# Prompt attention with probabilities split into two fp16 parts by VectorE instead of fp32 words split and rejoined around a DMA transpose

## The chip, the cores and the metric

The kernel runs on one core of a Trainium2 chip. The metric is the device time of one execution in microseconds (us). A lower time is better. The profile shows one execution, with the busy intervals of TensorE (PE; its weight loads are PEld), VectorE (DVE), ScalarE (ACT), GpSimd (POOL), and the DMA queue that SyncE issues (SP).

## What is computed

One layer of a hybrid trunk over two groups of requests with shared weights: a prompt of 1024 tokens and eight samples of 16 tokens. After a modulated RMS norm, one projection gives q, k, v, gates and the inputs of a state-space branch (SSD). The change touches the attention of the prompt alone:

```python
def attend(q, k, v, bias, mask):
    s = jnp.einsum('bqhd,bkhd->bhqk', q, k).astype(jnp.float32) * (ATT_HEAD_DIM ** -0.5) + bias[None].astype(jnp.float32)
    s = jnp.where(mask, s, -1e30)
    p = jax.nn.softmax(s, axis=-1).astype(v.dtype)
    return jnp.einsum('bhqk,bkhd->bqhd', p, v)
```

There are 16 heads of 64 columns. A chunk of 64 query tokens sees itself and the 8 chunks before it, so a block of 128 queries works with at most 5 blocks of 128 keys. The output of attention is gated and projected, the SSD branch runs on the same normed input, both are merged, projected and added to the input.

## The kernel before

All 1152 tokens (1024 of the prompt, 128 of the samples) are worked through together. Large products are made from fp16 parts: an fp32 operand becomes a high part `hi` and a rest `lo`, and three fp16 matmuls replace one in fp32 (hi x hi, hi x lo, lo x hi). `halves` makes the parts (ScalarE the high one, VectorE the rest), and `level` sums squares of an operand into a column of `sums`. At the end every column is compared with a range; if one is outside, a flag makes the program run a second, general kernel behind this one.

The program is emitted by one loop, `run`. Its main stream are dense projections, in matmuls that stream 384 columns (`dense`, lines 409 to 412, and `dense_tok`, lines 462 to 464). Between them it puts the steps of other generators when a planned clock (`clock[0]`) and credits let them go; `until(t)` and `pause(t)` hold a generator to a planned time, and `late(...)` keeps an instruction in program order. Instructions of one engine run in their order; the hardware waits on semaphores.

Attention has 8 units of two heads each (`attention(u)`). A unit projects q, k, v for all tokens (`dense_gen`, evicted by `ev`), normalises and transposes q and k (`prelude`), and then runs `prompt` and `sample`. `prompt` has eight query blocks `m` of 128 tokens with `n = min(m, 4) + 1` key blocks, in six rounds (`ROUNDS`). A round first multiplies finished probabilities with v (`weigh`, line 1057), and then makes scores (line 1101) for one to three query blocks into PSUM; the two-bank tile `s` exists once, the one-bank tiles `g` three times. VectorE evacuates the scores with the bias and a running minimum (`negated`, line 1007). ScalarE exponentiates and sums (`exps`, line 1001). VectorE makes the reciprocal (line 1002) and scales the probabilities in fp32 (line 1004).

The probabilities must be transposed, keys onto partitions. `turn(m)` does it with the DMA transpose, which moves 2-byte elements: ScalarE copies the fp32 words into two planes of 16-bit halves (line 1034), the DMA transposes both planes (line 1036), and VectorE joins them to fp32 words again (line 1041). `weigh` then runs one fp32 matmul for each key block and head, with 64 columns of `v` as weights; the two heads write the two halves of the PSUM partitions. VectorE multiplies the result into the gate (line 1107). The sample's probabilities go through the same three steps (lines 1174, 1175, 1177).

Buffers are slots of one SBUF arena, by layouts: `L_ATT` for attention (tag "S" holds 10 buffers of 640 columns for scores and what is transposed, tag "T" whole rows of v and gates), `L_SSD` and `L_HEAD` for the SSD stage, and `L_MORE`, six further row buffers from column `E0` on, which SSD stages take first. `walloc` and `wpair` hold a generator until a slot is free.

Of the kernel before, what the change touches and what calls it, by code (L numbers as in the profile page):

```python
# [9 lines left out]
F16 = mybir.dt.float16  # L10
# [6 lines left out]
P = 128  # L17
# [42 lines left out]
SW = 2.0 ** 8  # L60
SA = 4.0
SM = 1.0
W_MEAN = (4.0, 1024.0)
X_MEAN = (0.25, 2.0 ** 19)

# [73 lines left out]
def trunk_kernel(ctx: ExitStack, tc: tile.TileContext, h, again):  # L139
# [80 lines left out]
    L_START["ada"] = L_START["ada"] + arena.set_layout(E0, [("ada", 8, 1024)])["ada"]  # L220
    L_MORE = arena.set_layout(E0, [("T", 6, 1184), ("H", 1, 1024)])
    L_SSD["H"] = L_SSD["H"] + L_MORE["H"]
    L_ST = rarena.set_layout(0, [("b", 4, P), ("s", 2, P), ("x", 2, 2 * P)])

    def alloc(lay, tag, cols):
        if lay is L_H or lay is L_W or lay is L_W3 or lay is L_Q:
# [654 lines left out]
    def attention(u):  # L881
# [4 lines left out]
        def dense_gen():  # L886
            qk = yield from walloc(lay, "Q", 16 * P)
            v = yield from walloc(lay, big, NT)
            nb = yield from walloc(lay, "n", 84)
            st["qk"], st["v"], st["nb"] = qk, v, nb  # L890
            if u == NU - 1:
                dts["raw"] = yield from walloc(lay, "T", NT)

            def ev(t, ps):

                while t == 8 and "turned" not in st:
                    blocked[0] = "q and k of the first tokens"
                    yield None
                c = qk.ap[:, 2 * (t % 8) * P:2 * (t % 8 + 1) * P]
                nc.scalar.activation(c, ps[:, :2 * P], AF.Copy, scale=1.0 / SW)  # L900
# [88 lines left out]
        def done():  # L989
            st["left"] -= 1  # L990
            att_left[0] -= 1
            if st["left"] == 0:
                dma(att_d[u], st["z"].ap)
                for n in ("z", "v"):
                    st[n].free()

        def exps(ps, sm_):

            n = len(ps)
            for e, p in enumerate(ps):  # L1000
                nc.scalar.activation(p, p, AF.Exp, bias=sm_[:, 4 + e:5 + e], scale=-1.0, accum_out=sm_[:, 6 + e:7 + e])  # L1001
            nc.vector.reciprocal(sm_[:, 8:8 + n], sm_[:, 6:6 + n])
            for e, p in enumerate(ps):
                nc.vector.tensor_scalar(p, p, sm_[:, 8 + e:9 + e], None, ALU.mult)  # L1004

        def negated(p, least, ps, bap, most=3.0e38):
            late(nc.vector.tensor_tensor_reduce(p, ps, bap, -1.0, most, ALU.add, ALU.min, least))  # L1007
# [1 line left out]
        def prompt():  # L1009
# [2 lines left out]
            qh, ql, kh, kl = st["ops"]  # L1012
            v, z, bias = (st[n] for n in ("v", "z", "bias"))

            place, turned, probs, tpt, mins = {}, {}, {}, {}, {}
            claimed = set()
            pairs = {0: 3, 1: 2, 2: 1, 3: 0}

            def turn(m):

                n = min(m, 4) + 1
                if pairs.get(m) in claimed:
                    yield from ready(lambda: m in turned)
                else:
                    claimed.add(m)
                    t = yield from wpair(lay, "S", 640)
                    for q, at in ((m, place[m][0][1]), (pairs.get(m), {0: 4 * P, 2: 2 * P}.get(pairs.get(m), 0))):
                        if q is not None:
                            turned[q] = [(b, at) for b in t]
                turning[0] -= 1  # L1030
                for e in range(2):
                    yield from until(probs[m] + 1000 * e)
                    (x, at), (y, _) = place[m][e], turned[m][e]
                    nc.scalar.activation(planes(y, at, n), words(x, at, n), AF.Copy)  # L1034
                    yield from until(probs[m] + 1000 * e + 900)
                    dma(x.ap[:, at:at + n * P].bitcast(U16).rearrange("p (i k) -> p i k", k=P),
                        y.ap[:, at:at + n * P].bitcast(U16), transpose=True)
                for e in range(2):
                    yield from until(probs[m] + 1000 * e + TURN)
                    (x, at), (y, _) = place[m][e], turned[m][e]  # L1040
                    nc.vector.tensor_copy(words(y, at, n), planes(x, at, n))  # L1041
                xs = place.pop(m)
                if pairs.get(m) not in place:
                    for x, _ in xs:
                        x.free()
                tpt[m] = clock[0] + 3500

            def weigh(js, po):

                cost = 200  # L1050
                for a, j in enumerate(js):
                    n = min(j, 4) + 1
                    for i in range(n):
                        for e in range(2):
                            vc = (j + 1 - n + i) * P + e * HD
                            x, o = turned[j][e]
                            late(nc.tensor.matmul(po[e * HD:e * HD + HD, a * P:(a + 1) * P], v.ap[:, vc:vc + HD],  # L1057
                                                  x.ap[:, o + i * P:o + (i + 1) * P], start=i == 0, stop=i == n - 1))
                    cost += 2 * n * 103
                for j in js:  # L1060
                    for x, _ in turned.pop(j):
                        if pairs.get(j) not in turned:
                            x.free()
                return cost

# [10 lines left out]
            for pieces, js in ROUNDS:  # L1076
# [27 lines left out]
                yield cost  # L1104
                if js:
                    ms = slice(js[0] * P, (js[-1] + 1) * P)
                    nc.vector.scalar_tensor_tensor(z.ap[:, ms], po, 0.5 / SW, z.ap[:, ms], ALU.mult, ALU.mult)
                t = clock[0] + 1000
                for m, c, w, k, o in pieces:
                    n = min(m, 4) + 1  # L1110
# [7 lines left out]
                    t += 4.4 * w  # L1118
                    if c + w == n * P:
                        exps([x.ap[:, at:at + n * P] for x, at in place[m]], sm_)  # L1120
                        mins.pop(m).free()
# [10 lines left out]
        def sample():  # L1132
# [6 lines left out]
            for bg in range(2):  # L1139
# [20 lines left out]
                    x.free()  # L1160
                negated(p.ap, sm_.ap[:, 4:5], sv[:, :640], bs.ap)
                exps([p.ap], sm_.ap)
                sm_.free()
                bs.free()
                yield 1400
# [2477 lines left out]
```

## Time and profile before

| | us |
|---|---|
| median of 3 runs | 1877.16 (1872.84 to 1878.64) |
| the profiled execution | 1871.97 |
| its span, first to last instruction | 1870.2 |
| TensorE busy in the span | 1781.9 (95%) |
| VectorE busy | 1210.7 (65%) |
| ScalarE busy | 1049.5 (56%) |

The mean granted TensorE clock was 0.991 of full speed. Matmuls are pipelined, so the busy time of a group of matmuls is the union of their intervals, and the duration of one contains its way through the array; the rate is seen from one start to the next. Idle time of an engine is put down to what released it last. A group's row gives line, engine, operation, tiles, shape and count, then busy us and mean ns of one, then the idle time before it.

### The profile page before, as it was taken

The page shows a single profiled execution, that of the slowest core. Times are in us where ns is not written, and L with a number is a line of the kernel's source. Part 1 is how long each engine was busy: PE and PEld are TensorE (multiplying, and loading weights), DVE is VectorE, ACT ScalarE, POOL GpSimd, SP SyncE. Part 2 cuts the span into 40 slices and gives each one's busy share as a digit, 9 for nine tenths or more (in the row PEclk, how much of TensorE's full clock was granted, in tenths as well). Part 3 has the DMA queues.
Part 4 walks back from the last instruction along what each step waited for, and adds up shares of the span by engine and source line. Part 5 has one row for each costly group of instructions (what it writes and reads, how often), then busy time and mean ns, then how long its engine had stood idle before and what let it go on. Part 6 is the DMA issues. An engine that isn't in the chain of part 4 may idle for free. (4 is left out here: it accounts for less than half of the span.)

```text
span 1870.2 us, 34169 instructions
## 1 busy us (share of the span) xinstructions
PE 1781.9 (95%) x13341; PEld 1114.3 (60%) x13341; DVE 1210.7 (65%) x2247; ACT 1049.5 (56%) x1999; POOL 350.0 (19%) x624
## 2 busy tenths in 40 slices
PE   7998998988989999999999999999999999999997
PEld 3655555554555555666666666566666656666664
DVE  7446657565675676776777787677664634888732
ACT  8866765666667667555655565465554623334520
POOL 0222313232232210121132213212212110000000
PEclk9999999999999999999999999999999999999999
DMA  9257767675676768453444435444456863331331
GB/s 382 92 125 191 157 178 171 173 178 149 166 194 176 168 150 181 128 168 104 120 152 140 134 116 159 127 127 122 136 168 207 325 205 97 109 97 46 98 123 53
DMA packets 266564, 284.84 MB, mean 152 GB/s; under 512 B 199628, under 2 KB 200664, under 8 KB 266392
## 3 DMA queue, kind: packets, MB, share of 16 engines
q1 hardware_dynamic: 257432, 253.90, 48.9%
q0 software_dynamic: 8960, 28.65, 4.0%
q8 instruction: 107, 1.75, 0.4%
q14 instruction: 65, 0.53, 0.1%
HBM read 192.70 MB, written 43.66 MB: 126 GB/s over the span
## 5 line engine op out<-in xcount | busy, mean ns | idle before, releaser
L409 PE MATMUL d<-arena 128*128 128x384 f16 x2172 | 711.4, 328 | 1.5 <-DVE arena L1408 1.3
L410 PE MATMUL d<-arena 128*128 128x384 f16 x2172 | 711.2, 327 | 0.0
L412 PE MATMUL d<-arena 128*128 128x384 f16 x2172 | 711.0, 327 | 0.0
L412 PEld LDWEIGHTS <-arena 128*128 128x128 f16 x2280 | 224.0, 98 | 148.2 <-issue 4.4
L409 PEld LDWEIGHTS <-arena 128*128 128x128 f16 x2280 | 223.9, 98 | 147.9 <-issue 10.5
L410 PEld LDWEIGHTS <-arena 128*128 128x128 f16 x2280 | 223.9, 98 | 142.7 <-issue 6.6
L319 ACT ACTIVATE arena<-arena 128x1024 bf16<-128x1024 f32 (+2 forms) x161 | 173.4, 1077 | 132.9 <-DMA arena<-in_wall_dram 109.9
L327 ACT ACTIVATE arena<-arena 128x1024 f16<-128x1024 f32 (+1 forms) x117 | 121.2, 1043 | 172.1 <-PE d L410 147.4
L1041 DVE COPY arena<-arena 128x1280 uint16<-128x1280 uint16 (+4 forms) x128 | 101.2, 791 | 140.6 <-DMA arena<-arena 125.6
L462 PE MATMUL d<-arena 128*128 128x384 f16 (+1 forms) x568 | 186.4, 329 | 1.9 <-ACT arena L665 1.6
L463 PE MATMUL d<-arena 128*128 128x384 f16 (+1 forms) x568 | 186.7, 329 | 0.0
L464 PE MATMUL d<-arena 128*128 128x384 f16 (+1 forms) x568 | 186.5, 329 | 0.0
L328 DVE SCALAR_TENSOR_TENSOR arena<-arena 128x1024 f16<-128x1024 f32 (+1 forms) x117 | 144.3, 1234 | 25.5 <-ACT arena L327 25.4
L1001 ACT ACTIVATE arena<-arena 128x640 f32<-128x640 f32 (+2 forms) x144 | 100.9, 703 | 102.8 <-DVE arena L1007 102.6
L1034 ACT ACTIVATE arena<-arena 128x1280 uint16<-128x1280 uint16 (+4 forms) x128 | 122.4, 995 | 46.2 <-DVE arena L1004 32.5
L1437 ACT ACTIVATE arena<-arena 128x128 f32<-128x128 f32 x288 | 88.3, 388 | 49.5 <-DMA arena<-acs_d 49.5
L1249 DVE SCALAR_TENSOR_TENSOR arena<-arena 128x1176 f32<-128x1176 f32 x72 | 104.6, 1453 | 5.6 <-ACT arena L1246 5.0
L928 POOL TENSOR_SCALAR arena<-arena 128x16 f32<-128x16 f32 (+1 forms) x24 | 8.5, 354 | 463.8 <-DVE arena L906 463.7
L1057 PE MATMUL g<-arena 128*64 128x128 f32 x960 | 67.9, 283 | 16.4 <-DVE arena L1041 7.6
L462 PEld LDWEIGHTS <-arena 128*128 128x128 f16 x576 | 56.7, 98 | 44.7 <-issue 9.8
L463 PEld LDWEIGHTS <-arena 128*128 128x128 f16 x576 | 56.4, 98 | 39.6 <-issue 5.2
L464 PEld LDWEIGHTS <-arena 128*128 128x128 f16 x576 | 56.5, 98 | 38.6 <-issue 2.5
(238 smaller groups left out, 2637.0 us busy)
## 6 DMA issues: line engine op xcount, KB each, us to landing
arena<-in_wall_dram SPq DMA_DIRECT2D x85, 512.0 KB
arena<-acs_d SPq DMA_DIRECT2D x32, 576.0 KB
arena<-in_kc_dram SPq DMA_DIRECT2D x64, 256.0 KB
arena<-in_vc_dram SPq DMA_DIRECT2D x64, 256.0 KB
arena<-in_wada_dram SPq DMA_DIRECT2D x24, 512.0 KB
arena<-in_xT_dram SPq DMA_DIRECT2D x16, 576.0 KB
gate_d<-arena POOLq DMA_DIRECT2D x48, 192.0 KB, 3.3
arena<-eacs_d SPq DMA_DIRECT2D x32, 288.0 KB
```

The source lines that it names most:

```text
L319: keep(nc.scalar.activation(junk[:, :n], x, AF.Square, scale=scale * n ** -0.5, accum_out=sums[:, c:c + 1]))
L327: keep(nc.scalar.activation(hi, x, AF.Copy, scale=scale))
L328: keep(nc.vector.scalar_tensor_tensor(lo, x, scale, hi, ALU.mult, ALU.subtract))
L409: nc.tensor.matmul(ps, hi.r[:, wc], kh.r[:, tok], start=k == 0, stop=False)
L410: nc.tensor.matmul(ps, hi.r[:, wc], kl.r[:, tok], start=False, stop=False)
L412: nc.tensor.matmul(ps, lo.r[:, wc], kh.r[:, tok], start=False, stop=k == nk - 1)
L462: nc.tensor.matmul(ps, kh.r[:, tok], wh, start=k == 0, stop=False)
L463: nc.tensor.matmul(ps, kh.r[:, tok], wl, start=False, stop=False)
L464: nc.tensor.matmul(ps, kl.r[:, tok], wh, start=False, stop=k == KT - 1)
L1034: nc.scalar.activation(planes(y, at, n), words(x, at, n), AF.Copy)
L1041: nc.vector.tensor_copy(words(y, at, n), planes(x, at, n))
L1249: nc.vector.scalar_tensor_tensor(yc, r.ap[:, j:j + n], w4[:, i, j:j + 1], yc, ALU.mult, ALU.add)
```

## The change

The scaling of the prompt's probabilities moves out of `exps` and into `turn`. There VectorE writes, for each head, the scaled probability times 2^12 as fp16 and the rest, computed in fp32 and rounded to fp16, behind it, into a second buffer; this buffer is transposed by DMA back into the one that held the fp32 scores. ScalarE's splitting copy and VectorE's joining copy are gone for the prompt; the sample keeps them. `weigh` runs three fp16 matmuls for each key block and head: high part of v with the high and the low part of the probabilities, low part of v with the high part. The fp16 parts of v are made in `ev` (by `halves`, in two pieces of 512 columns) and checked by `level`, which gives the range check eight more entries. They lie in a new layout `L_V`, 4 slots of 512 columns from `E0` on; four more buffers of tag "S" lie behind them, both over slots of `L_MORE`. The planned times in `turn` and the planned cost in `weigh` change with it.

```diff
-    NPART, NOPER = 121, 40
+    NPART, NOPER = 121, 48
...
+    L_V = arena.set_layout(E0, [("v", 4, NP // 2)])
+    L_ATT["S"] = L_ATT["S"] + arena.set_layout(E0 + 4 * NP // 2, [("S", 4, 640)])["S"]
...
+                if t in (4, 8):
+                    o = slice((t - 4) * P, t * P)
+                    halves(vh.r[:, o], vl.r[:, o], v.ap[:, o], 1.0)
+                    if t == 8:
+                        level(vh.r, 1.0, kind="x")
...
         def exps(ps, sm_):
-            n = len(ps)
             for e, p in enumerate(ps):
                 nc.scalar.activation(p, p, AF.Exp, bias=sm_[:, 4 + e:5 + e], scale=-1.0, accum_out=sm_[:, 6 + e:7 + e])
-            nc.vector.reciprocal(sm_[:, 8:8 + n], sm_[:, 6:6 + n])
-            for e, p in enumerate(ps):
-                nc.vector.tensor_scalar(p, p, sm_[:, 8 + e:9 + e], None, ALU.mult)
...
             def turn(m):
...
+                sm_ = mins.pop(m)
+                r = sm_.ap[:, 8:10]
+                yield from until(probs[m] - 1000)
+                nc.vector.reciprocal(r, sm_.ap[:, 6:8])
+                nc.vector.tensor_scalar(r, r, SP, None, ALU.mult)
+                ys = []
                 for e in range(2):
-                    yield from until(probs[m] + 1000 * e)
-                    (x, at), (y, _) = place[m][e], turned[m][e]
-                    nc.scalar.activation(planes(y, at, n), words(x, at, n), AF.Copy)
-                    yield from until(probs[m] + 1000 * e + 900)
-                    dma(x.ap[:, at:at + n * P].bitcast(U16).rearrange("p (i k) -> p i k", k=P),
-                        y.ap[:, at:at + n * P].bitcast(U16), transpose=True)
+                    x, at = place[m][e]
+                    p = x.ap[:, at:at + n * P]
+                    y = temp[m][e].ap[:, at:at + n * P].bitcast(F16)
+                    nc.vector.tensor_scalar(y[:, :n * P], p, r[:, e:e + 1], None, ALU.mult)
+                    nc.vector.scalar_tensor_tensor(y[:, n * P:], p, r[:, e:e + 1], y[:, :n * P], ALU.mult, ALU.subtract)
+                    ys.append(y)
+                sm_.free()
                 for e in range(2):
-                    yield from until(probs[m] + 1000 * e + TURN)
-                    (x, at), (y, _) = place[m][e], turned[m][e]
-                    nc.vector.tensor_copy(words(y, at, n), planes(x, at, n))
...
-                tpt[m] = clock[0] + 3500
+                    yield from until(probs[m] + 1000 + 1400 * e)
+                    x, at = place[m][e]
+                    dma(x.ap[:, at:at + n * P].bitcast(U16).rearrange("p (i k) -> p i k", k=P), ys[e].bitcast(U16), transpose=True)
+                yield from until(probs[m] + 2400 + TURN)
...
+                tpt[m] = clock[0]
...
             def weigh(js, po):
...
                     for i in range(n):
-                        for e in range(2):
-                            vc = (j + 1 - n + i) * P + e * HD
-                            x, o = turned[j][e]
-                            late(nc.tensor.matmul(po[e * HD:e * HD + HD, a * P:(a + 1) * P], v.ap[:, vc:vc + HD],
-                                                  x.ap[:, o + i * P:o + (i + 1) * P], start=i == 0, stop=i == n - 1))
-                    cost += 2 * n * 103
+                        o = slice((j + 1 - n + i) * P, (j + 2 - n + i) * P)
+                        for w, (v_, b) in enumerate(((vh, i), (vh, n + i), (vl, i))):
+                            for e in range(2):
+                                late(nc.tensor.matmul(po[e * HD:e * HD + HD, a * P:(a + 1) * P], v_.r[:, o.start + e * HD:o.start + e * HD + HD],
+                                                      xs[e][:, b * P:(b + 1) * P], start=i == 0 and w == 0, stop=i == n - 1 and w == 2))
+                    cost += n * 165
...
-                    nc.vector.scalar_tensor_tensor(z.ap[:, ms], po, 0.5 / SW, z.ap[:, ms], ALU.mult, ALU.mult)
+                    nc.vector.scalar_tensor_tensor(z.ap[:, ms], po, 0.5 / (SW * SP), z.ap[:, ms], ALU.mult, ALU.mult)
```

`SP` is 2^12. The sample's code scales its probabilities itself now, with the two instructions that stood in `exps`.

More of the change, by code (lines that the diff above doesn't have):

```diff
@@ L62 @@
 SM = 1.0
+SP = 2.0 ** 12
 W_MEAN = (4.0, 1024.0)
@@ L889, in dense_gen @@
             nb = yield from walloc(lay, "n", 84)
-            st["qk"], st["v"], st["nb"] = qk, v, nb
+            vh = yield from walloc(L_V, "v", NP)
+            vl = yield from walloc(L_V, "v", NP)
+            st["qk"], st["v"], st["nb"], st["v16"] = qk, v, nb, (vh, vl)
             if u == NU - 1:
@@ L1013, in prompt @@
             v, z, bias = (st[n] for n in ("v", "z", "bias"))
-            place, turned, probs, tpt, mins = {}, {}, {}, {}, {}
-            claimed = set()
+            vh, vl = st["v16"]
+            place, temp, probs, tpt, mins = {}, {}, {}, {}, {}
+            claimed, turned = set(), set()
             pairs = {0: 3, 1: 2, 2: 1, 3: 0}
@@ L1021, in turn @@
                 n = min(m, 4) + 1
[L1022 to L1025, printed above, removed]
+                if m not in claimed:
                     t = yield from wpair(lay, "S", 640)
-                    for q, at in ((m, place[m][0][1]), (pairs.get(m), {0: 4 * P, 2: 2 * P}.get(pairs.get(m), 0))):
-                        if q is not None:
-                            turned[q] = [(b, at) for b in t]
+                    for q in {m, pairs.get(m, m)}:
+                        claimed.add(q)
+                        temp[q] = t
@@ L1162, in sample @@
                 exps([p.ap], sm_.ap)
+                nc.vector.reciprocal(sm_.ap[:, 8:9], sm_.ap[:, 6:7])
+                nc.vector.tensor_scalar(p.ap, p.ap, sm_.ap[:, 8:9], None, ALU.mult)
                 sm_.free()
```

19 lines of the change are left out of this document (10 added, 9 removed).

## The prediction

> **What bounds the kernel now.** I read the page's head first, then the busy time by windows, split about where the attention ends. The columns are the stretch, its length, busy time of TensorE, weight loads, VectorE, ScalarE and GpSimd with instruction counts, granted clock, DMA share, GB/s.
>
> ```profile
> span 1870.2 us, 34169 instructions
> ...
> PE 1781.9 (95%) x13341; PEld 1114.3 (60%) x13341; DVE 1210.7 (65%) x2247; ACT 1049.5 (56%) x1999; POOL 350.0 (19%) x624
> ```
> ```profile
> 100.00:745.00 645.00, 588.81 (x4984) 350.73 (x4983) 409.89 (x1033) 426.92 (x889) 157.92 (x283) 0.98 0.69 168
> 745.00:1870.20 1125.20, 1106.13 (x7774) 713.00 (x7772) 744.89 (x1132) 542.90 (x963) 173.95 (x302) 1.00 0.44 136
> ```
> ```profile
> 466.00:473.50 7.50, 6.24 (x40) 3.86 (x40) 6.40 (x14) 5.27 (x7) 6.93 (x8) 0.54 0.82 180
> 673.00:745.00 72.00, 66.20 (x567) 41.11 (x566) 50.40 (x104) 52.44 (x88) 7.72 (x15) 1.00 0.67 156
> ```
>
> TensorE is the bound throughout, so whatever is taken from its work or its idle time moves the end. After 745 us it idles 19 us in 1125; during attention 645 - 588.8 = 56.2 us, and there the clock is 0.98 of full, worth 0.02 x 645 = 13 us. The loss comes in short pieces: from 466 to 473.5 us the clock was 0.54, right behind a wait. The waits show what TensorE waited for (total, times, longest):
>
> ```profile
> PE s L1101 <- DVE arena L1007: 18.0, 8, 3.2
> PE g L1186 <- ACT arena L900: 7.7, 4, 2.8
> PE g L1057 <- DVE arena L1041: 7.6, 6, 2.6
> ```
>
> The first is a score matmul that finds its PSUM bank not yet emptied by VectorE. The timeline shows one, and that it runs slowly afterwards: the same six score matmuls start 0.75 us before the next six here, 0.42 us in an undisturbed round.
>
> ```profile
> 306.58 0.33 PE L412 MATMUL d<-arena 128*128 128x384 f16 x1
> 306.75 0.33 PE L409 MATMUL d<-arena 128*128 128x384 f16 x1
> 309.55 0.98 PE L1101 MATMUL s<-arena 64*128 64x320 f16 x6 [2.48 <-DVE arena L1007]
> 310.30 1.04 PE L1101 MATMUL g<-arena 64*128 64x320 f16 x6
> ...
> 397.14 0.58 PE L1101 MATMUL s<-arena 64*128 64x320 f16 x6
> 397.56 0.57 PE L1101 MATMUL g<-arena 64*128 64x320 f16 x6
> ```
>
> **The products on TensorE.** Per pair of heads there are 1+2+3+4+4x5 = 30 blocks of 128 keys, 240 in all. Before, a block is one fp32 matmul for each head, in two halves of the array's columns at once, four records a block. The groups by form:
>
> ```profile
> L1057 PE MATMUL g<-arena 128*64 128x128 f32 x960 | 67.9, 283 | 16.4 <-DVE arena L1041 7.6 <-issue 4.1 <-DVE arena L1007 2.3
> ...
> L1545 PE MATMUL g<-arena 128*64 128x16 f32 x512 | 17.8, 207 | 0.0
> ```
> ```profile
> 366.98 0.75 PE L1101 MATMUL s<-arena 64*128 64x128 f16 x12
> 367.57 0.57 PE L1101 MATMUL g<-arena 64*128 64x320 f16 x6
> ```
>
> 67.9 us / 240 = 0.283 us a block, with the ends of the runs. After, a block is six fp16 matmuls, three pairs. No fp16 matmul with 64 weight columns is in the trace, so I bound a pair. From below: in the last fence twelve matmuls, six of 128 columns and six of 320, take 367.57 - 366.98 = 0.59 us; six of 320 take 0.42 (above), so three pairs of 128 columns take 0.17, 0.057 a pair. From above: L1545 has the weight shape of the change (128x64, two column halves) and next to nothing to stream; 17.8 us / 256 pairs = 0.070, which is what two such weight loads cost by themselves. I take 0.065, as the load is the nearer row: 0.195 a block, 0.22 with the ends of runs, 53 us in all, **15 us less**. Bounds 0.19 and 0.24: 22 and 10 less.
>
> The Trainium skill speaks against this: "TensorE: Matmul & The Clock Gate", section "Back-to-back issue gap", gives about 81 ns for each matmul of 128 columns in a stream of weight loads and matmuls. By it a block would be 6 x 0.081 = 0.49 us and the products an estimated 49 us longer. The pairs of 0.057 us above do not agree with it as long as two halves of the array overlap.
>
> **Work moved between VectorE and ScalarE.** Rows of the page and of the groups by form:
>
> ```profile
> L1041 DVE COPY arena<-arena 128x1280 uint16<-128x1280 uint16 (+4 forms) x128 | 101.2, 791 | 140.6 <-DMA arena<-arena 125.6
> ...
> L1034 ACT ACTIVATE arena<-arena 128x1280 uint16<-128x1280 uint16 (+4 forms) x128 | 122.4, 995 | 46.2 <-DVE arena L1004 32.5
> ```
> ```profile
> L328 DVE SCALAR_TENSOR_TENSOR arena<-arena 128x1024 f16<-128x1024 f32 x113 | 138.5, 1227 | 24.9 <-ACT arena L327 24.8
> L319 ACT ACTIVATE arena<-arena 128x1024 bf16<-128x1024 f32 x117 | 123.3, 1054 | 132.2 <-DMA arena<-in_wall_dram 109.9 <-DMA arena<-in_wssd_dram 10.7 <-DMA arena<-in_watt_dram 7.1
> L1001 ACT ACTIVATE arena<-arena 128x640 f32<-128x640 f32 x80 | 65.6, 820 | 85.6 <-DVE arena L1007 85.5
> L1631 DVE SCALAR_TENSOR_TENSOR arena<-arena 128x1152 f16<-128x1152 f32 x32 | 43.3, 1365 | 4.2 <-ACT arena L1629 4.2
> L1004 DVE TENSOR_SCALAR arena<-arena 128x640 f32<-128x640 f32 x80 | 41.4, 551 | 1.5
> L1007 DVE CUSTOM_DVE_ANT_0 arena<-g,arena 128x320 f32<-128x320 f32 x48 | 24.5, 544 | 0.0
> L1007 DVE CUSTOM_DVE_ANT_0 arena<-s,arena 128x320 f32<-128x320 f32 x48 | 21.4, 484 | 0.1
> L1002 DVE RECIPROCAL arena<-arena 128x2 f32<-128x2 f32 x64 | 10.2, 159 | 39.9 <-ACT arena L1001 39.9
> L1564 DVE TENSOR_TENSOR arena<-arena 128x512 f32<-128x512 f32 x16 | 11.0, 689 | 0.3
> ```
>
> ScalarE loses L1034, 122 us. It gains 16 fp16 copies of v of 512 columns (at most the 1.05 us of L319, 17 us) and 8 squares of 1024 (8.4 us): some 97 us less over the stage's 427. VectorE loses the copies behind the transpose, 101 us. It keeps the scaling (L1004, now writing fp16) and gains 128 subtractions. L328 and L1631 give (1365 - 1227)/128 = 1.08 ns an element, so 0.81 us at 640 columns and 0.26 to 0.68 at 128 to 512: 64 x 0.81 + 16 x 1.87 = 82 us. With 64 more tiny operations (0.16 each, 10 us) and 16 subtractions for v (0.69, 11 us) VectorE comes out 2 us up: no gain, no loss. The DMA transposes stay, as many and as large; their source is now written by VectorE, and TensorE waits for their landing itself.
>
> **Idle time.** In the built order of TensorE's instructions I count the 384-column dense matmuls (306.58 and 306.75 above are two in a row; the kernel plans 0.1625 us for one) between two uses of the score bank. Before, prompt scores follow sample scores by 44 and 22 of them; the 22 (3.6 us) is where 309.55 waits. After, it is 38 and 87. The tightest new distance is 18, from the scores of query block 7 to the next sample scores. So of the 18 us I let 15 go. L1057's wait for the copies goes, as the copy does; except in the last pair of heads the products come 81 or more dense matmuls (13 us) behind the scores that they need, more than the chain of 10.2 us worked out below: 6.5 of 7.6. The wait for L900 shrinks with ScalarE's load: 5 of 7.7. Together **26 us**, between 0 and 33. What is late next is VectorE's queue, where the scaling and subtraction of one block, 2 x (0.55 + 0.81) = 2.7 us, now stand between evacuations. With half of the longest waits gone, I let half of the clock loss go: **7 us** (0 to 13).
>
> **What the change costs: the last pair of heads.** The fp16 parts of v and four more score buffers lie where the first SSD tiles go. In the built order the dense matmuls run out there: after the scores of block 5 only 41 dense matmuls precede its products, and none stands between the scores of block 7 and the products of blocks 6 and 7 (before: 85 and 57). The chain then lies open. Its DMA part:
>
> ```profile
> 288.46 2.63 SPq L1036 DMA_TRANSPOSE arena<-arena  x2
> ...
> 291.78 0.75 DVE L1041 COPY arena<-arena 128x1024 uint16<-128x1024 uint16 x1 [1.20 <-DMA arena<-arena]
> 292.98 2.47 DVE L1041 COPY arena<-arena 128x1024 uint16<-128x1024 uint16 x1 [0.46 <-DMA arena<-arena]
> ```
>
> Two issues take 2.63 us and the second lands 292.98 - 291.09 = 1.9 us later. For block 7: evacuation 2 x 0.48 + 2 x 0.54 = 2.1; exponentials to 1.4 us later (the first of two of 0.82 overlaps the evacuation); reciprocal and scaling factor 0.3; scaling and first subtraction 2 x 0.55 + 0.81 = 1.9; issues 2.6 and landing 1.9: 10.2 us idle. Block 5 has 41 x 0.1625 = 6.7 us of dense matmuls and about 3 of others as cover: some 2 us idle. A wait three times the 3.2 us ahead of the window at 466 us costs at least its loss, 0.46 x 7.5 = 3.4 us; I take 3. In all **15 us more** (10 to 20); the 5.8 us that TensorE idles from 673 to 745 us today (72 - 66.2) are left as they are.
>
> **Sum.** -15 - 26 - 7 + 15 = -33 us. The profiled execution took 1872.0 us (span 1870.2 and 1.8 around it), so 1839 by its own time; the median of the runs shown is 1877.2, so **1844 us** there. Favourable ends: -22 - 33 - 13 + 10 = -58, 1819. Unfavourable: -10 - 0 - 0 + 20 = +10, 1887. A measurement of this kernel cannot tell less than about 0.3%, 5.6 us, from no change.
>
> **Rivals.** *The idle time does not fall.* VectorE stays first in, first out and 410 us busy of 645; the new reciprocals still wait for exponentials (39.9 us in L1002's row), and new waits replace the old ones. Then -15 + 15 = 0: 1877, give or take 10. For it: VectorE's load is unchanged. Against: 125.6 us of its waiting for transposes (L1041's row) go.
>
> *Slower: the halves of the array do not overlap in fp16.* Each of the six matmuls of a block then takes a pair's time, 6 x 0.065 = 0.39 us, 94 us for 240, 26 more instead of 15 less: -33 + 41 = +8, 1885, and with the upper bound of 0.07, 1892. The point from which it decides: the products alone lose above 0.283/3 = 0.094 us a pair, the whole change above (67.9 + 18)/240/3 = 0.119. Against it: in L1057 and L1545 the halves overlap in fp32.
>
> The Trainium skill, "TensorEngine Tiling", section "Restrictions and Gotchas", says that column tiling excludes fast weight load, which is one way to this rival. No run here shows fp16 weights in column halves.
>
> *The change does not do what it says.* Its range check gets eight more entries, one for each v; if one failed, the second kernel in the program would run as well, which at least doubles the time.
>
> **Chances.** Forecast 0.62; idle time unchanged 0.26; slower products 0.10; second kernel 0.02. Nearly all of the forecast and half of the second case are faster by over 0.3%: 0.75. Of the rest of the second case 0.08 lies within 0.3% and 0.05 above; with the last two, 0.17 slower. The range goes from 1816 to 1878 us: it leaves out little below and 0.18 above.
>
> **What would show it.** The products' group at 45 to 58 us busy; ScalarE near 950 us, VectorE near 1213; the wait of score matmuls for evacuation below 5 us; TensorE's idle time in attention below 45 us, with one piece of about 10 us ahead of the last products and a half clock behind it. Wrong if the products' group is over 68 us, or if new waits of TensorE on VectorE or DMA in the first seven units sum to over 20 us.

## The result and the profile after

The changed kernel takes 1844.18 us in the median of four runs (1841.84 to 1849.27); the kernel before, on the same chip, 1875.0 (1871.91 to 1878.64). The ratio is 0.984, with a 95% interval of 0.981 to 0.987. The forecast was 1844.0. The profiled execution took 1841.84 us at a mean clock of 0.991. Its head, the busy time by windows, and the waits of TensorE from 100 to 760 us (lines behind the change have moved: 1057 is now 1070, 1101 is 1115, 1155 is 1168, 1186 is 1201):

```profile
span 1839.7 us, 35020 instructions
...
PE 1770.4 (96%) x13821; PEld 1105.9 (60%) x13821; DVE 1229.7 (67%) x2327; ACT 958.6 (52%) x1903; POOL 330.0 (18%) x624
```
```profile
100.00:620.00 520.00, 502.68 (x4797) 295.11 (x4795) 371.81 (x997) 286.31 (x703) 129.13 (x264) 1.00 0.75 183
```
```profile
100.00:745.00 645.00, 609.11 (x5709) 363.60 (x5708) 457.71 (x1162) 357.93 (x851) 144.76 (x293) 0.98 0.72 177
...
620.00:700.00 80.00, 61.95 (x575) 37.90 (x575) 50.76 (x109) 39.73 (x78) 7.39 (x16) 0.85 0.65 159
```
```profile
PE g L1070 <- DMA arena<-arena: 10.7, 6, 5.6
PE s L1115 <- DVE arena L1013: 6.3, 6, 1.3
PE g L1201 <- DVE arena L1192: 6.1, 6, 1.7
PE g L1070 <- DVE arena L1013: 3.7, 1, 3.7
```

From 100 to 745 us TensorE idles 645 - 609.1 = 35.9 us, where it idled 56.2. Half of that lies in the last of the eight pairs of heads, now from 620 to 700 us: 80 - 61.95 = 18 us, at a clock of 0.85 (673 to 745 before: 5.8 us at 1.00). The seven pairs ahead of it ("regular" below) idle 520 - 502.7 = 17 us at a clock of 1.00, where they idled 50. The timeline of the last pair shows the pieces; the number in brackets is the idle time ahead:

```profile
655.44 3.41 PE L1070 MATMUL g<-arena 128*64 128x128 f16 x60 [3.67 <-DVE arena L1013]
...
667.65 0.28 PE L1070 MATMUL g<-arena 128*64 128x128 f16 x1 [5.63 <-DMA arena<-arena]
668.99 1.81 PE L1070 MATMUL g<-arena 128*64 128x128 f16 x29 [1.05 <-DMA arena<-arena]
673.24 0.31 PE L1070 MATMUL g<-arena 128*64 128x128 f16 x1 [2.44 <-DMA arena<-arena]
674.33 0.96 PE L1070 MATMUL g<-arena 128*64 128x128 f16 x14 [0.78 <-DMA arena<-arena]
```

The groups that moved most are the products, the new subtraction, and, which nobody had forecast, the sample's score matmuls. Their row before is the last one:

```profile
L1070 PE MATMUL g<-arena 128*64 128x128 f16 x1440 | 50.6, 228 | 14.4 <-DMA arena<-arena 10.7 <-DVE arena L1013 3.7
L1168 PE MATMUL s<-arena 128*32 128x512 f32 x128 | 36.2, 635 | 5.1 <-DMA arena<-in_kc_dram 2.6 <-issue 2.2 <-DVE arena L1013 0.2
L1046 DVE SCALAR_TENSOR_TENSOR arena<-arena 128x640 f16<-128x640 f32 x64 | 55.2, 879 | 0.0
```
```profile
L1155 PE MATMUL s<-arena 128*32 128x512 f32 x128 | 18.1, 605 | 0.2 <-DVE arena L1007 0.2
```

A ledger of TensorE's time makes the sum exact. Each matmul is counted from its start to the next start, or to its own end where that comes first; what lies between is idle (us; the sample scores are two lines of code, against the loaded keys and the sample's own; the last four rows are experiments told below).

| kernel | products | sample scores | dense | all other | idle | sum |
|---|---|---|---|---|---|---|
| before | 64.9 | 20.4 | 1416.6 | 280.0 | 72.1 | 1854.0 |
| after | 49.3 | 38.5 | 1405.1 | 277.5 | 53.1 | 1823.5 |
| third product left out | 34.2 | 35.0 | 1409.2 | 279.0 | 63.2 | 1820.7 |
| keys by GpSimd's queue | 52.9 | 26.3 | 1413.1 | 280.8 | 80.8 | 1853.8 |
| parts of v moved up | 46.0 | 33.2 | 1411.7 | 276.2 | 47.2 | 1814.3 |
| moved up, keys early and together | 46.9 | 19.6 | 1414.5 | 282.9 | 61.2 | 1825.1 |

Before to after: products -15.6, idle -19.0, dense -11.5 (the same 8568 matmuls: less time at half clock, and fewer ends of runs, whose last matmul counts whole when a wait follows: 49 such ends before, 11 after), sample scores +18.1, other -2.5: -30.5. The question that the experiments had to answer is which of these terms set the end.

### The profile page after: what moved, and what is told of

It reads as the page before. It is cut to its first block, busy times and chain, and to the rows that moved or that the text cites. A ratio compares the mean times of both kernels' runs of the same rounds, so it can differ in the third digit from the quotient of the medians.

```text
span 1839.7 us, 35020 instructions
## 1 busy us (share of the span) xinstructions
PE 1770.4 (96%) x13821; PEld 1105.9 (60%) x13821; DVE 1229.7 (67%) x2327; ACT 958.6 (52%) x1903; POOL 330.0 (18%) x624
## 5 line engine op out<-in xcount | busy, mean ns | idle before, releaser
L322 ACT ACTIVATE arena<-arena 128x1024 bf16<-128x1024 f32 (+3 forms) x169 | 181.8, 1076 | 144.3 <-DMA arena<-in_wall_dram 122.1
L331 DVE SCALAR_TENSOR_TENSOR arena<-arena 128x1024 f16<-128x1024 f32 (+1 forms) x117 | 148.9, 1273 | 53.2 <-ACT arena L330 53.0
L1010 ACT ACTIVATE arena<-arena 128x640 f32<-128x640 f32 (+3 forms) x144 | 100.9, 703 | 122.4 <-DVE arena L1013 122.3
L1046 DVE SCALAR_TENSOR_TENSOR arena<-arena 128x640 f16<-128x640 f32 (+4 forms) x128 | 87.4, 713 | 0.0
L1514 POOL TENSOR_TENSOR rarena<-rarena,arena 128x256 fp32r<-128x256 f32 x64 | 55.3, 878 | 73.8 <-PE g L1598 50.2
L1534 DVE SCALAR_TENSOR_TENSOR arena<-arena,g 128x64 f32<-128x64 f32 x224 | 46.4, 275 | 32.6 <-ACT arena L1530 30.6
```

Of the source, the lines that this page charges most:

```text
L322: keep(nc.scalar.activation(junk[:, :n], x, AF.Square, scale=scale * n ** -0.5, accum_out=sums[:, c:c + 1]))
L331: keep(nc.vector.scalar_tensor_tensor(lo, x, scale, hi, ALU.mult, ALU.subtract))
```

## The experiments

**The products.** One of three products of each block is left out, so the output lacks v's low part.

```diff
-for w, (v_, b) in enumerate(((vh, i), (vh, n + i), (vl, i))):
+for w, (v_, b) in enumerate(((vh, i), (vh, n + i))):
...
-                                                      xs[e][:, b * P:(b + 1) * P], start=i == 0 and w == 0, stop=i == n - 1 and w == 2))
+                                                      xs[e][:, b * P:(b + 1) * P], start=i == 0 and w == 0, stop=i == n - 1 and w == 1))
```

> The changed kernel without the third product of each block (the low part of v by the high part of the probabilities is left out; transfers, VectorE and ScalarE as before it). The trace of after has 1440 of these matmuls in 50.6 us, 228 of which is the mean length of one, with starts 28.9 ns apart. Theory (the products lie on TensorE's path, their cost is their number times 28.9 ns): 480 fewer, about 34 us for the group and about 14 to 17 us off the time, 1828 to 1831. Rival (the products stand beside waits that end later anyway, for the transposed probabilities or VectorE): the group falls to 34 us, TensorE's idle time in the attention grows by as much, and the time falls by less than 5 us.

Measured: 1837.12 us (1835.8 to 1841.54), 7.1 below after; ratio to before 0.980 (0.976 to 0.983). Group and waits:

```profile
L1070 PE MATMUL g<-arena 128*64 128x128 f16 x960 | 35.8, 226 | 8.8 <-DVE arena L1219 3.6 <-DMA arena<-arena 3.1 <-DVE arena L1121 2.1
```
```profile
PE s L1168 <- DMA arena<-in_kc_dram: 8.7, 6, 2.0
PE s L1115 <- DVE arena L1013: 8.5, 5, 2.2
PE d L412 <- DVE arena L1423: 5.8, 1, 5.8
```

The group lost 14.8 us, the time 7.1. Between the two theories: the rest came back as idle time, 10.1 us in the ledger. A unit with less TensorE work arrives sooner at things that do not get sooner: the sample's keys (2.6 to 8.7 us), the scores' evacuation (6.3 to 8.5), and once 5.8 us in a dense projection.

**The order of the products.** The loops over `w` and `e` are exchanged: three products of one head, then three of the other.

> The changed kernel with the products of each block in another order: the three of the first head, then the three of the second, where the two heads' products alternated. The work is the same. Trace of after: 1440 matmuls start 28.9 ns apart, a pair in 57.8 ns. Theory (two products in different column halves run beside each other, one behind another in the same half doesn't): the starts lie 40 to 57 ns apart on average, the time rises by 15 to 40 us, 1859 to 1884. Rival (the rate is that of a single fp16 matmul of this size wherever it is placed): the starts stay at 29 ns and the time within 4 us of 1844.

Measured: 1848.5 us (1847.33 to 1849.79), 4.3 above after; the products do not move:

```profile
L1070 PE MATMUL g<-arena 128*64 128x128 f16 x1440 | 50.9, 228 | 14.9 <-DMA arena<-arena 9.4 <-DVE arena L1013 3.7 <-DVE arena L1121 1.8
```

By the numbers the rival is all but right (it allowed 4 us), but the starts do not bear out its reason. They still come in pairs, 10 and 46 ns apart, where the alternating order gives 3 and 53: 56 ns a pair in both. A dense matmul of 384 columns starts 163 ns behind the one before it, so 128 columns are worth 54 ns by estimate: a pair takes the time of one. The second record to start carries the wait for the second head's transposed probabilities, which by the source belongs to the fourth matmul. So the two halves still run beside each other, and the other head's first product started ahead of two that stand before it in the source. Whether TensorE took it out of order or the build had put it there, the trace does not tell; so what two products of one half would cost behind each other was not tried.

**VectorE's queue and ScalarE's load.** Three kernels, two from after, one from before. In the first the reciprocals and the making of the parts go back behind the exponentials:

```diff
-                yield from until(probs[m] - 1000)
                 nc.vector.reciprocal(r, sm_.ap[:, 6:8])
```

> The changed kernel with the reciprocals and the making of the fp16 parts put on VectorE's queue right behind the exponentials' issue, where the changed kernel puts them at the planned time of the exponentials' end. Trace: the wait of the prompt's score matmuls for VectorE's reading of earlier scores was 18.0 us before and is 6.3 us after. Theory (a reciprocal that waits for ScalarE's exponential holds up the reading of scores behind it, and putting it later took 12 us off TensorE's idle time): that wait goes back to 14 us or more, and the time rises by 8 to 20 us, 1852 to 1864. Rival (the wait fell because ScalarE has 91 us less to do and the exponentials come sooner): it stays below 9 us, the time within 4 us of 1844.

Measured: 1846.96 us (1845.26 to 1851.87), 2.8 above after, with runs that overlap those of after.

```profile
PE s L1114 <- DVE arena L1013: 5.5, 5, 1.5
```

The theory falls for the changed kernel: the wait is no longer than it was. The same part alone, put into the kernel before (reciprocal and fp32 scaling move from `exps` to `turn`, behind `until(probs[m] - 1000)`):

> The kernel before, with one part of the change alone: reciprocals and scaling of the prompt's probabilities leave the place right behind the exponentials and stand at the planned time of their end, as in the changed kernel; fp32 words, copies and products stay. Theory (a wait of score matmuls for VectorE, 18.0 us before, comes from reciprocals that wait at the head of VectorE's queue): that wait falls below 9 us and the time by 6 to 14 us, 1861 to 1869. Rival (undoing the same part in the changed kernel cost only 2.8 us, so the waits fell with ScalarE's work and the steps taken out of the chain): the wait stays above 12 us and the time within 5 us of 1875.

Measured: 1868.71 us (1866.35 to 1872.49), ratio 0.9958 (0.9942 to 0.9974), 8.2 less than before beside it (1876.88).

```profile
PE g L1105 <- ACT arena L1197: 7.7, 5, 4.4
PE g L1061 <- DVE arena L1045: 7.5, 8, 2.2
PE s L1105 <- DVE arena L1003: 7.1, 6, 1.9
```

Here the wait (the last line) does fall, 18.0 to 7.1, and the time by 8 us, by the interval 5 to 11; the theory holds for the kernel before. Part of the wait moved: the other score bank now waits 7.7 us for ScalarE, and counted like the ledger's, TensorE's idle time falls by 5.0 us in all. ScalarE's load put back on top of after, two copies behind each pair of parts:

```diff
+                for e in range(2):
+                    yield from until(probs[m] + 1000 * e)
+                    nc.scalar.activation(junk[:, :n * P], ys[e][:, :n * P], AF.Copy)
+                    nc.scalar.activation(junk[:, :n * P], ys[e][:, :n * P], AF.Copy)
```

> The changed kernel with two copies of each fp16 part pair added on ScalarE, into a scratch tile that nobody reads: 256 copies, which put back about the 91 us of ScalarE work that the change took away (958.6 back to about 1050 us busy). Theory (ScalarE's relief is worth little, the place of the reciprocals on VectorE's queue is what shortened the waits): time within 6 us of 1844. Rival (TensorE's idle time fell with ScalarE's load): the idle time of the attention goes from 36 back to 50 us or more and the time rises by 12 to 30 us, 1856 to 1874.

Measured: 1856.0 us (1854.45 to 1859.32), 11.8 above after, with ScalarE at 1088 us, 129 more and not 91.

```profile
PE g L1074 <- DMA arena<-arena: 13.1, 6, 5.2
PE g L1205 <- DVE arena L1196: 11.8, 5, 3.8
PE g L1217 <- ACT arena L1211: 8.1, 5, 1.9
```

Nearer to the rival, though TensorE's idle time from 100 to 745 us comes to 48.3 us and not to the 50 that it named. Scaled to the 91 us that the change took away, 11.8 x 91/129 is an estimate of 8 us. So ScalarE, busy half of the time and never the bound, was worth about as much as the place of the reciprocals, by waits of TensorE that stand behind it. The copies also wait at the head of ScalarE's queue for VectorE (11 us in all), as the splitting copy did; load and wait were not separated. The two gains do not add: with ScalarE relieved the place is worth 2.8 at most, without it 8.2. How the rest of the gain splits between the joining copy that is gone and the other order of the steps was not separated.

**The last pair of heads.** The same work, with v's parts and the four score buffers placed higher, so that more of the next stage's rows are free:

```diff
-    L_V = arena.set_layout(E0, [("v", 4, NP // 2)])
-    L_ATT["S"] = L_ATT["S"] + arena.set_layout(E0 + 4 * NP // 2, [("S", 4, 640)])["S"]
+    L_V = arena.set_layout(E0 + 6 * 1184, [("v", 4, NP // 2)])
+    L_ATT["S"] = L_ATT["S"] + arena.set_layout(E0 + 6 * 1184 - 4 * 640, [("S", 4, 640)])["S"]
```

> The changed kernel with the two fp16 parts of v and the added score buffers moved up in the arena, so that fewer of the places that the next stage fills while the last heads are at work are theirs; the work is the same. Trace of after: the last pair of heads (620 to 700 us) has 18.0 us of TensorE idle and 23.9 us at half clock, the regular pairs of heads no half clock at all. Theory (the last pair is laid open because the work that should cover it can't have its places): idle there falls below 9 us, the half-clock stretches there go, and the time falls by 12 to 24 us, 1820 to 1832. Rival (the last pair waits for VectorE and the transfers whatever lies beside it): idle there stays above 14 us and the time within 4 us of 1844.

Measured: 1833.01 us (1831.0 to 1834.92), ratio 0.977 (0.974 to 0.981), 11.2 below after.

```profile
620.00:700.00 80.00, 69.84 (x669) 42.69 (x668) 54.77 (x120) 46.82 (x93) 7.80 (x19) 1.00 0.78 194
```

The cause holds; both sizes just miss the theory's bounds (idle below 9 us, time at most 1832). From 620 to 700 us TensorE idles 10.2 instead of 18.0 us, and the clock is 1.00 instead of 0.85: the 180 products there, from start to start, take 6.2 us instead of 9.4. These 8 us of idle time and 3 of products are as much as the 11 us that reach the end. The rest of the ledger moved too (dense +6.6, sample scores -5.3, idle time elsewhere +2, others -1) and about cancels.

**The sample's keys.** In the ledger the sample scores look like a loss of 18 us. Two timelines of one such group, after and before:

```profile
224.18 1.04 PE L1168 MATMUL s<-arena 128*32 128x512 f32 x2
225.16 0.66 PE L962 MATMUL g<-arena 128*128 128x128 f32 x4
225.74 1.92 PE L1168 MATMUL s<-arena 128*32 128x512 f32 x4
228.25 0.62 PE L1168 MATMUL s<-arena 128*32 128x512 f32 x1 [0.59 <-DMA arena<-in_kc_dram]
228.70 0.59 PE L1168 MATMUL s<-arena 128*32 128x512 f32 x1
```
```profile
301.08 1.07 PE L1155 MATMUL s<-arena 128*32 128x512 f32 x8
```

Eight records of four column groups take 1.07 us when all stand ready. After, the second group of seven units takes 3.0 to 5.1: transposes of q and k stand between its first matmul and the others, and its keys come one at a time, loaded on SyncE's queue behind DMA transposes that wait for VectorE. First the loads alone, moved to GpSimd's queue:

```diff
-                    dma(kc.ap, h["kc"][u, 4 * bg + i])
+                    store(kc.ap, h["kc"][u, 4 * bg + i])
```

> The changed kernel with the loads of the sample's keys issued on GpSimd's queue instead of SyncE's, where they stand behind the transposing transfers that wait for VectorE. Trace of before: the 128 sample score matmuls take 18.1 us; of after: 36.2 us, since the keys come one at a time and the four column groups no longer run together. Theory (late keys, held in SyncE's queue): the group falls back to 18 to 22 us, the wait of the weight loads for the keys from 12.1 to below 4 us, and the time falls by 8 to 18 us, 1826 to 1836. Rival (the matmuls run one after the other because of where they stand between other work, or because each one waits for its own load wherever it is issued): the group stays above 30 us and the time within 4 us of 1844.

Measured: 1871.2 us (1862.04 to 1878.91), 27 above after, although the group falls to 24.3 us (the trace is of an execution of 1878.91):

```profile
PE g L1070 <- DMA arena<-arena: 30.7, 13, 5.5
PE g L1201 <- issue: 8.1, 5, 3.6
```

Both theories miss. The new wait is for the transposes of the probabilities. Two timelines of SyncE's queue tell when these are through: the bias load (L953) goes into a place that transposes ahead of it still read, and the waits name them as what it waits for. Here, with GpSimd's issue of the keys below it, and in after:

```profile
434.33 6.51 SPq L1052 DMA_TRANSPOSE arena<-arena  x4
450.09 0.33 SPq L953 DMA_DIRECT2D arena<-in_bias_dram  x1
```
```profile
439.03 2.22 POOL L1158 DMA_DIRECT2D arena<-in_kc_dram  x4 [9.91 <-PE g L1201]
```
```profile
425.95 6.26 SPq L1052 DMA_TRANSPOSE arena<-arena  x4
436.33 0.33 SPq L953 DMA_DIRECT2D arena<-in_bias_dram  x1
```

From the last transpose's issue to the bias load: 436.33 - 432.21 = 4.1 us in after, 450.09 - 440.84 = 9.3 with 1 MB of keys under way beside them. This unit has the longest such stretch in both kernels. In all seven units it is 2.1 to 4.1 us in after (2.5 on average) and 5.1 to 9.3 with the keys on GpSimd's queue (7.0). The wait of that load, after first:

```profile
SPq L953 <- DMA arena<-arena: 17.4, 7, 4.0
```
```profile
SPq L953 <- DMA arena<-arena: 48.9, 7, 9.2
```

SyncE's order, which made the keys late, also kept them out of the transposes' way. With both edits, places and GpSimd's queue:

> The changed kernel with both: the sample's keys loaded over GpSimd's queue, and the parts of v with the added score buffers moved up in the arena. Theory (two costs at different places, each on TensorE's path): the two gains add, 20 to 40 us, 1804 to 1824. Rival (the same waiting is counted twice): the time is that of the better of the two alone, within 4 us.

Measured: 1855.01 us (1853.15 to 1859.4). The places give their part again (-16), the queue takes its own (+22); the products wait 24.1 us for transposes. Neither theory holds; nothing is won by the keys. On top of the moved places, the sample's scores were then planned 4 us later (`pause(4500)` to `pause(8500)`):

> The kernel with the parts of v and the added score buffers moved up in the arena (1833.0 us), and with the sample's score matmuls placed 4 us later behind the issue of their keys (planned pause 4.5 to 8.5 us); queues and transfers as before. Theory (the four column groups run one by one because their keys come one by one just as TensorE gets to them; 36.2 us for the group in after, 31.2 in the kernel that this one starts from): the group falls to 18 to 25 us without a new wait, and the time falls by 5 to 12 us, 1821 to 1828. Rival (the keys or the transposes of the probabilities are late for whatever is placed there, since the DMA engines are full in these stretches): the group falls but the waits of the products for the transposes grow by as much, and the time stays within 3 us of 1833 or rises.

Measured: 1831.95 us (1829.85 to 1833.52), 1.1 less than without; the group stays at 31.4 us. The groups start no later than without the pause (150.6 against 152.1 us, 222.8 against 228.2), so this told nothing of the cause. Next, again from the kernel with the moved places, eight places for keys and values instead of four, so that the loads stand ahead of the transposes; two of the four added score buffers are given up for them:

```diff
-    L_ATT["S"] = L_ATT["S"] + arena.set_layout(E0 + 6 * 1184 - 4 * 640, [("S", 4, 640)])["S"]
+    L_ATT["S"] = L_ATT["S"] + arena.set_layout(E0 + 6 * 1184 - 2 * 640, [("S", 2, 640)])["S"]
+    L_ATT["K"] = L_ATT["K"] + arena.set_layout(E0 + 6 * 1184 - 2 * 640 - 4 * 512, [("K", 4, 512)])["K"]
```

> The kernel with the parts of v moved up in the arena (1833.0 us), with eight places instead of four for the sample's keys and values (two of the four added score buffers are given up for them). The keys of a unit's second sample group can then be loaded while the values of the first are still in use, and in the issue order of SyncE's queue they come ahead of the probabilities' transposes instead of behind and between them. Trace of the kernels so far: the first group of a unit takes TensorE 1.07 us, the second 2.6 to 5.1 us in after, because its first keys are there and its last are not. Theory (late keys, for want of places): the whole group falls from 31 to about 18 us, the transposes are not disturbed, and the time falls by 8 to 13 us, 1820 to 1825. Rival (TensorE's longer group filled time in which it would have waited for the transposes): the group falls to 18 us, the waits of the products for the transposes rise from 4.4 by about as much, time within 4 us of 1833.

Measured: 1840.49 us (1833.37 to 1844.19), 7.5 above the kernel with the moved places. The group falls to 23.6 us, the second one of six units still at 2.62. The products' wait for transposes, without and with the eight places (the trace of the eight places is of an execution of 1833.37 us):

```profile
PE g L1070 <- DMA arena<-arena: 4.4, 5, 2.2
```
```profile
PE g L1071 <- DMA arena<-arena: 8.7, 10, 1.7
```

The waits go the rival's way, but the time rises by more than its 4 us; how much of that the two missing score buffers cost was not tried. One edge of issue order, the first score matmul of a group behind the last transpose of q and k, alone and with the eight places:

> The kernel with the parts of v moved up in the arena (1833.0 us), with one edge in the issue order: a sample group's first score matmul is put behind the transposes of q and k that its unit's next steps need, so that these no longer stand between the first and the other three. In after and in the kernels so far the built order has them there in the second group of six units, and such a group can't take TensorE less than 2.6 us (against 1.07 us) even when all keys are there. The keys still come one by one. Theory (order and late keys each cost TensorE about a microsecond and a half to two a group): the group falls from 31 to about 23 us, the time by 4 to 9 us, 1824 to 1829. Rival (TensorE's longer group only fills time in which it would wait a little later for the sample's probabilities or the prompt's transposes): the group falls, the waits grow as much, time within 4 us of 1833.

Measured: 1838.57 us (1834.99 to 1843.05), 5.6 above the kernel without the edge. The group is at 33.3 us and waits 4.5 us for the keys instead of 2.3, so neither theory was put to the test.

> The same edge in the kernel with eight places for the sample's keys and values (1840.5 us): keys early and the four matmuls of a group together. Theory: the group is back at 17 to 19 us as before the change, 13 us less than in the kernel that it starts from, and the time comes out 8 to 13 us below 1833, 1820 to 1825. Rival (what the group gives back, other waits take, the transposes of the probabilities above all, since the values' loads now stand between these on SyncE's queue): the waits of the products for the transposes stay at 8 us or more, and the time stays at 1829 or above.

Measured: 1844.31 us (1837.75 to 1848.61), with the sample scores entirely as before the change. Their group, and one unit by windows, in this kernel and in the one with the moved places alone:

```profile
L1174 PE MATMUL s<-arena 128*32 128x512 f32 x128 | 17.0, 604 | 4.2 <-issue 4.2
```
```profile
340.00:415.00 75.00, 69.46 (x680) 42.23 (x676) 50.50 (x138) 39.25 (x96) 17.82 (x37) 0.95 0.75 181
```
```profile
340.00:415.00 75.00, 71.43 (x687) 42.43 (x685) 52.09 (x139) 40.07 (x96) 17.87 (x37) 1.00 0.79 186
```

By its numbers the rival is right (8.5 us of waits for transposes, time above 1829). Of the 14 us of TensorE's time nothing reached the end: the kernel is 11 us slower than the one with the moved places, TensorE idles 14 us more, and in this unit, with longer waits, the clock is 0.95 instead of 1.00. The edits have prices of their own, though: the edge alone came with 5.6 us, the eight places with 7.5. Against the kernel with the eight places alone, where only the edge differs, the sample scores fall from 25.7 to 19.6 us, counted as in the ledger, and the time is 3.8 higher, with runs that overlap. So no run got faster by giving the sample's scores their time back. That they were slow in time in which TensorE would otherwise have stood still fits all of them; a run that gives the time back and changes nothing else is missing. What is shown is that a matmul that waits inside its group counts as busy, and that the 18 us in the ledger can't be read as a cost.

The best kernels of all are the two with the moved places, 1833.0 and 1832.0 us; both beat the changed kernel and the one before.

## Why the prediction was right

The sum came out within a microsecond of the median. Its terms:

| step | forecast | measured |
|---|---|---|
| products | -15 | -19 at full clock (64.9 to 46.1 in the ledger, without the 3.2 that the last pair's half clock adds) |
| idle time, regular pairs | -26 | -33; by the ledger 18 came back as waiting inside the sample's groups: -15 |
| clock, regular pairs | -7 | about -8 (dense matmuls in a row: 9.0 us over 163 ns each before, 2.5 now; score matmuls 88.2 to 85.5 ns, 529 of them) |
| last pair of heads | +15 | about +17 (idle +12, clock 3.2 on products, 1 on dense, some on scores) |
| not forecast | | about -6 (ends of dense runs, others) |

- **Products.** A pair takes 56 ns: the lower bound of 57, from the row of the score matmuls, not the 65 that leaned to the weight loads; these take 115 ns each and lie beside the matmuls. The Trainium skill's 81 ns for each matmul ("TensorE: Matmul & The Clock Gate", "Back-to-back issue gap") does not hold here: in the regular pairs the starts lie 27.9 ns apart on average, 30.0 with the last pair (the expectations above say 28.9). That the whole term lies on the path was assumed, and is not shown: leaving out another 14.8 us brought 7.1.
- **Idle time.** The step holds in size, its parts less so. L1101's wait fell by 11.7 and not by 15; L1057's for the copies and L1186's for L900 went altogether; L1201's for VectorE's copies of the sample came new (6.1), and with 2.6 for the keys and 0.8 for the transposes the new waits of the seven regular pairs stay well below the 20 us that would have refuted the step. The reason given, more dense matmuls between two uses of the score bank, was not tried by itself. In the kernel before, the place of the reciprocals on VectorE's queue, which the prediction did not price, took L1101's wait from 18.0 to 7.1 alone, as far as the whole change did, and 8 us off the time. ScalarE's load, priced at 5, was worth an estimate of 8. So the size of the step came out, and the reason given for its largest part is not shown. And some idle time became matmuls that wait inside their group, which the prediction did not think of.
- **Last pair of heads.** The pieces ahead of the last products sum to 5.63 + 1.05 + 2.44 + 0.78 = 9.9 us for the forecast 10.2, all at the transposes, but in four pieces where one was forecast. The products of blocks 4 and 5 waited 3.67 us for the forecast 2, for VectorE's evacuation. That the places cause most of it, the moved places show: 8 of the 12 us of idle time go, and so does the half clock.
- **VectorE, +2**: +19; no run shows what that cost at the end. A subtraction of 640 columns takes 879 ns, not 813, and the tiny scaling of the reciprocals 206, not 160. **ScalarE, -97**: -91.
- **Left out**: the sample. The built order puts transposes of q and k into its score groups, and its keys come late behind the transposes on SyncE's queue. Neither was foreseen, and no run that mended either got faster by it.

The two larger misses, 4 too little on products and 11 too much on idle time once the sample's groups are counted in, stand against each other and the -6 that no step named; the hit within a microsecond is partly luck. Of the rivals, unchanged idle time and halves that do not overlap are refuted by the rows above, and one execution of the program shows no second kernel. Of what was to be seen, the products, ScalarE and the idle time of attention (35.9) lie in their bounds; the wait of the score matmuls, 6.3 us, is above the 5 given, and VectorE's 1230 above 1213.

## What to carry to other kernels

In a program whose order is fixed, work taken from the bounding engine is worth its time only as far as what it waits for next is also ready: here half for the products, and nothing in any run for the sample's scores. Before a group that grew is called a cost, give it its old time back in one run, and change nothing else in it. And memory that a change takes from the next stage is a cost of its own, at the place where that stage should cover the last chain: moving the buffers was worth a third as much again as the whole change.

## What the runs showed of the hardware

- Products in the two column halves of the array overlap in fp16: 56 ns a pair of 128 columns, where 163 ns for a dense matmul of 384 columns make an estimate of 54 for a single one. With three of one half ahead of three of the other in the source, the rate was the same and the starts still came in pairs (10 and 46 ns); what put them in that order is open.
- DMA transposes were through 2.1 to 4.1 us after the last issue in seven units, and 5.1 to 9.3 us with 1 MB of loads from another queue beside them. Moving these loads from SyncE's to GpSimd's queue delayed the transposes.
- Equal idle time can go with a very different clock: 18 us in the last 80 us of attention, with single waits up to 5.6 us, went with a clock of 0.85; 17 us spread over the 520 us before, in waits of at most 1.7 us, with 1.00. Whether the length of the waits or their closeness does it was not separated.
